# The MLP's down product: half its columns by one level of Strassen's scheme, between the blocks of the next up product

## The chip, the cores and the metric

The kernel runs on one core of one Trainium2 chip. A core has TensorE (PE) for matmuls, VectorE (DVE), ScalarE (ACT) and GpSimd (POOL) for the rest, and SyncE (SP), which issues most transfers. Each engine works through its own list of instructions in order and waits for others through semaphores. Matmul results go to PSUM, eight banks of 512 float32 columns on 128 partitions, from where DVE or ACT must copy them out; everything else lives in SBUF. The metric is the time of one execution in microseconds (us).

## The reference

Two decoder layers over 256 tokens of width 2048, each with a token mixer (mLSTM in layer 0, gated DeltaNet in layer 1), cross-attention into 256 memory tokens, and an MLP; each part stands between two RMS norms and is added to the residual. The change is in the MLP:

```python
D_MODEL = 2048; SEQ = 256; D_FF = 4 * D_MODEL        # 8192 features

def sq_relu_mlp(h, w_up, w_down):
    u = jax.nn.relu(h @ w_up)
    return (u * u) @ w_down

        h = rms_norm(x, g[4])
        x = x + rms_norm(sq_relu_mlp(h, w_up[i], w_down[i]), g[5])
```

## The kernel before

All matmuls run in fp32r, a reduced float32 format. To keep float32 accuracy every operand is split into a high part (a cast to fp32r) and a low part (the rest), and a product is three matmuls: high x high, high x low, low x high. Weights come from HBM as float32 (`raw`), in units of 128 x 2048 numbers; ACT makes `hi` by a cast (L101) and DVE makes `lo` by a subtraction (L102), each in two halves of 128 x 1024. The class `Weights` holds the list of all units in the order of their use (`plan`). When a unit is taken, those up to two further on are begun; there are three buffers each of `hi` and `lo` and four half-unit buffers of `raw`, so a unit's cast waits until the unit three before it has been used up by TensorE, and its transfer until a `raw` half is free.

A feature is a row of the hidden layer. The up product makes feature blocks of 128 features x 256 tokens (`prod_feat`, keys `up`): 16 blocks of the width are contracted, each by one matmul of 512 columns (L363: weights' high part against the high and low parts of `h` side by side) and one of 256 (L369: low part against high). Four feature blocks stand in four PSUM banks at once. Their evacuation (`relu2`, then `join`) is ACT copy `h_up` (L498), DVE addition `j_up` (L500), DVE relu and square in one (L1030), ACT cast (L264) and DVE subtraction (L265) into `u`.

The down product (`prod_tok`, key `down`) goes the other way: 128 tokens at a time are the stationary operand, 512 output columns the moving one, with three matmuls for each feature block, token half and column group (L437 to L439). There are four column groups, `y0` to `y3`. The MLP works in NQ = 4 chunks of 2048 features: up for the chunk, then down for the chunk, whose result is added to `y` (L557). A short extra matmul (`apart`, L365) stands between one chunk's down and the next one's up. The last chunk's down product runs inside `out_proj` (layer 0) or with the output's stores (layer 1), where the closing norm, the residual and, in layer 0, the first products of the next stage are woven in.

PSUM banks come in two kinds: five buffers of `acc` and three of `ps` (functions `acc` and `psum`). The order on each engine is set by the order of the code, with the splits of weights moved ahead by priority, and a scheduler that places each instruction.

Of the kernel before, what the change touches and what calls it, by code (L numbers as in the profile page):

```python
# [25 lines left out]
GDN_QKV, GDN_Z = 8192, 4096  # L26
XA_H, XA_DH = 4, 128
D_FF = 8192
NQ = 4
FQ = D_FF // NQ  # L30
COL_MEM, COL_HEAD, COL_GDN, COL_CONV = 192, 208, 224, 256
SOLVE_FROM = 6


class Weights:
# [10 lines left out]
    def add(self, key, w, k0, kn, n0, nn, tall=False):  # L46


        kk, un = (kn, P) if tall else (UK * P, UN)
        for n in range(n0, n0 + nn, un):  # L50
            w_n = min(un, n0 + nn - n)
            for k in range(k0, k0 + kn, kk):
                self.plan.append((key, w[k : min(k + kk, k0 + kn), n : n + w_n]))

    def begin(self, place=None):


        nc = self.nc
        if self.done == len(self.plan):
            return []  # L60
        key, src = self.plan[self.done]
        k, n = src.shape
        kb, i = k // P, self.done
        un = UN * UK // kb
        hi, lo, tiles, halves = [], [], [], []

        def take_tiles():
            if place:
                for j in range(kb):
                    for to, t in zip((hi, lo), place(j)):  # L70
                        to.append(t)
                return
            tiles.append(self.hi.tile([P, kb, un], F32R, tag="hi", name=f"hi{i}"))
            tiles.append(self.lo.tile([P, kb, un], F32R, tag="lo", name=f"lo{i}"))
            for to, t in zip((hi, lo), tiles):
                to += [t[:, j, :] for j in range(kb)]

        hb = kb // 2
        for k0 in range(0, kb, hb):
            raw = self.raw.tile([P, hb, un], F32, tag="raw", name=f"raw{i}_{k0}")  # L80
            nc.sync.dma_start(raw[:, :, :n], src[k0 * P : (k0 + hb) * P, :].rearrange("(kb p) n -> p kb n", p=P))

            def split(follow=None, k0=k0, raw=raw):
                if k0 == 0:
                    take_tiles()
                if not place:
                    ht, lt = tiles
                if kb == KB and n < P:
                    h_, l_ = ht[:, k0 : k0 + hb, 0:n], ht[:, k0 : k0 + hb, n : 2 * n]
                    a = nc.scalar.copy(h_, raw[:, :, :n])  # L90
                    return a, nc.vector.tensor_tensor(l_, raw[:, :, :n], h_, ALU.subtract)
                if place:
                    for j in range(hb):
                        h_ = hi[k0 + j][:, :n]
                        a = nc.scalar.copy(h_, raw[:, j, :n])
# [5 lines left out]
                a = nc.scalar.copy(h_, raw[:, :, :n])  # L101
                return a, nc.vector.tensor_tensor(l_, raw[:, :, :n], h_, ALU.subtract)  # L102

            halves.append(split)
        self.ready.append((key, hi, lo, kb, n))
        self.done += 1
        return halves

    def prefetch(self, n):
        while self.done < min(len(self.plan), self.taken + n):  # L110
            for half in self.begin():

                with self.tc.high_priority(offset=self.first):
                    ins = half()
                if self.splits is not None:
                    self.splits.append(ins[1])

    def take(self, key, ahead=None):
# [9 lines left out]
def trunk(ctx: ExitStack, tc, x, mem, norm_g, mem_norm_g, w_mem_kv, w_xq, w_xo, w_up, w_down,  # L128
# [87 lines left out]
    def acc(name):  # L216
        return ps.tile([P, 512], F32, tag="acc", bufs=5, name=name)
# [291 lines left out]
    def new_u(n=KB):  # L509
        return [acts.tile([P, 2 * T], F32R, tag=f"u{k}", name=f"u{k}") for k in range(n)]  # L510
# [23 lines left out]
    class Post:  # L534
# [105 lines left out]
        def split(self, half):  # L640
            self.order(*half(self.order))
# [382 lines left out]
        V.scalar_tensor_tensor(s2, s2, EPS, s2, ALU.mult, ALU.mult)  # L1024
        return s2

    def relu2(u):
        def ev_up(f, a):
            d = join(a, "up")
            V.scalar_tensor_tensor(d, d, 0.0, d, ALU.max, ALU.mult)  # L1030
            if f == 0:
                u.extend(new_u())
            split_into(u[f], d)

        return ev_up

    def mlp(l, lead):
        h = lead.h
        for c in range(NQ):
            u = []  # L1040
            prod_feat("up", h, KB, relu2(u), lead=None if c else lead, apart=last_of_down if c else None)
            if c == 0:
                post = Post(l, 5, (1, 0) if l == 0 else None)
            if c < NQ - 1:
                last_of_down = prod_tok("down", u, 4, lambda ch, t, a: post.add(ch, t, a, c == 0))
# [12 lines left out]
        prod_tok("down", u, 4, last, split=True)  # L1058
# [485 lines left out]
```

## Time and profile before

| what | value |
|---|---|
| median of 3 runs | 2859.65 us (2859.62 to 2866.31) |
| span of the profiled execution | 2861.4 us (the page gives no other total of it) |
| TensorE busy | 2837.7 us, 99% of the span |
| DVE busy | 1775.2 us, 62% |
| ACT busy | 1447.6 us, 51% |
| mean granted TensorE clock | 0.997 |
| MLP of layer 0, of layer 1 | 507 to about 1195 us, 2150 us to the end |
| moved by DMA | 562.31 MB, mean 197 GB/s |

A row of groups has: line, engine, operation, output <- inputs, shapes, count | busy us in all, mean ns of one | idle time of the engine just before them, and what ended it. A row of the timeline has: start, length, engine, line, operation. Lengths of matmuls overlap, so their rate is read from starts.

### The profile page before, as it was taken

What the parts mean: (1) busy time and instruction counts of PE and PEld (TensorE: products, weight loads), DVE (VectorE), ACT (ScalarE), POOL (GpSimd) and SP (SyncE); (2) the same over time, 40 slices, a digit from 0 to 9 for tenths busy, and PEclk for the clock granted to TensorE, in tenths of its full rate; (3) what the DMA queues carried; (4) which work ended last, traced back from release to release, by engine and by line L of the source; (5) the groups of instructions that cost most, each with busy time, mean ns of one, the idle gap of its engine ahead of it and who ended that gap; (6) DMA issues with size and microseconds to landing.
All of it is one profiled execution on the core that took longest, in us unless ns stands there. A gap on an engine that the chain in (4) does not pass through costs nothing.

```text
span 2861.4 us, 41169 instructions
## 1 busy us (share of the span) xinstructions
PE 2837.7 (99%) x15876; PEld 2426.8 (85%) x15876; DVE 1775.2 (62%) x2715; ACT 1447.6 (51%) x2201; POOL 170.3 (6%) x365
## 2 busy tenths in 40 slices
PE   9999999999999999999999999999999999999998
PEld 8888888888888888888888998888888888888887
DVE  6555657754645555687877895555577545555565
ACT  7354547644434444466765554544476444344443
POOL 0000000000000000002211114230000000000000
PEclk9999999999999999999999999999999999999999
DMA  8545565555555666658878778665655655656664
GB/s 281 182 148 176 188 201 172 167 191 191 191 192 191 191 191 191 218 158 233 245 217 227 209 219 262 196 202 197 208 160 177 189 193 190 193 190 192 192 191 155
DMA packets 379860, 562.31 MB, mean 197 GB/s; under 512 B 24672, under 2 KB 158640, under 8 KB 378384
## 3 DMA queue, kind: packets, MB, share of 16 engines
q1 hardware_dynamic: 362304, 505.02, 56.7%
q0 software_dynamic: 16464, 53.58, 5.8%
q8 instruction: 124, 2.03, 0.3%
q10 hardware_dynamic: 896, 1.09, 0.1%
q14 instruction: 72, 0.59, 0.1%
HBM read 534.38 MB, written 25.23 MB: 196 GB/s over the span
## 4 chain that ended last, share of the span: by engine, by line
PE 85%; DMA 5%; DVE 4%; ACT 4%; issue 2%; POOL 0%; DVEq 0%; ACTq 0%; SPq 0%; POOLq 0%
PE up L363 15%; PE down L437 8%; PE down L438 8%; PE down L439 8%; PE up L369 8%; PE gv L386 2%; PE o L363 2%; PE g_out L438 2%; PE g_out L439 2%; PE g_out L437 2%; ACT hi L101 2%; PE gz L437 1%; PE gz L439 1%; PE gz L438 1%; DVE lo L102 1%
## 5 line engine op out<-in xcount | busy, mean ns | idle before, releaser
L102 DVE TENSOR_TENSOR lo<-raw,hi 128x1024 fp32r<-128x1024 f32 (+1 forms) x924 | 1096.5, 1220 | 821.9 <-ACT hi L101 820.8
L101 ACT CAST hi<-raw 128x1024 fp32r<-128x1024 f32 (+1 forms) x924 | 932.5, 1049 | 905.3 <-PE down L439 311.1
L363 PE MATMUL up<-h,hi 128*128 128x512 f32 x1952 | 678.0, 392 | 1.5 <-DVE j_up L500 1.5
L369 PE MATMUL up<-h,lo 128*128 128x256 f32 x1952 | 544.9, 280 | 0.7 <-DVE lo L102 0.6
L363 PEld LDWEIGHTS up<-h,hi 128*128 128x128 f32 x1952 | 364.9, 187 | 81.8 <-issue 2.1
L439 PE MATMUL down<-hi,u 128*128 128x512 f32 x1024 | 398.5, 389 | 0.0
L438 PE MATMUL down<-lo,u 128*128 128x512 f32 x1024 | 398.5, 389 | 0.0
L437 PE MATMUL down<-hi,u 128*128 128x512 f32 x1024 | 398.4, 389 | 0.0
L369 PEld LDWEIGHTS up<-h,lo 128*128 128x128 f32 x1952 | 368.7, 189 | 3.0 <-DVE lo L102 2.3
L437 PEld LDWEIGHTS down<-hi,u 128*128 128x128 f32 x1024 | 192.2, 188 | 40.0
L439 PEld LDWEIGHTS down<-hi,u 128*128 128x128 f32 x1024 | 192.2, 188 | 40.0
L438 PEld LDWEIGHTS down<-lo,u 128*128 128x128 f32 x1024 | 192.2, 188 | 39.7
L437 PE MATMUL gz<-hi,h 128*128 128x512 f32 x256 | 103.0, 402 | 0.0
L439 PE MATMUL gz<-hi,h 128*128 128x512 f32 x256 | 102.4, 400 | 0.0
L438 PE MATMUL gz<-lo,h 128*128 128x512 f32 x256 | 102.4, 400 | 0.0
L1104 DVE SCALAR_TENSOR_TENSOR cv<-pad,cols,cv 128x256 f32<-128x256 f32 x192 | 92.0, 481 | 15.7 <-ACT cv L1102 12.3
L386 PE MATMUL gv<-h,hi 128*128 128x512 f32 x256 | 89.5, 394 | 0.0
L386 PE MATMUL gk<-h,hi 128*128 128x512 f32 x256 | 89.0, 392 | 0.0
L363 PE MATMUL o<-h,hi 128*128 128x512 f32 x256 | 89.0, 391 | 0.0
L264 ACT CAST u<-j_up 128x256 fp32r<-128x256 f32 x128 | 48.9, 406 | 57.9 <-DVE j_up L1030 57.9
L390 PE MATMUL gv<-h,hi 128*128 128x256 f32 x256 | 72.8, 284 | 0.0
L498 ACT COPY h_up<-up 128x256 f32<-128x256 f32 x128 | 47.1, 368 | 50.5 <-PE up L369 48.2
(473 smaller groups left out, 4582.5 us busy)
## 6 DMA issues: line engine op xcount, KB each, us to landing
raw<-in_w_up SPq DMA_DIRECT2D x256, 512.0 KB, 4.0
raw<-in_w_down SPq DMA_DIRECT2D x256, 512.0 KB, 4.5
raw<-in_gdn_w_in SPq DMA_DIRECT2D x192, 512.0 KB, 5.0
raw<-in_mlstm_w_in SPq DMA_DIRECT2D x96, 512.0 KB, 4.0
raw<-in_gdn_w_out SPq DMA_DIRECT2D x64, 512.0 KB, 4.7
raw<-in_mlstm_w_out SPq DMA_DIRECT2D x32, 512.0 KB, 4.7
at_d<-at POOLq DMA_DIRECT2D x8, 1536.0 KB, 7.6
ab<-at_d POOLq DMA_DIRECT2D x16, 768.0 KB, 5.0
```

The lines of the kernel that those rows point to most:

```text
L101: a = nc.scalar.copy(h_, raw[:, :, :n])
L102: return a, nc.vector.tensor_tensor(l_, raw[:, :, :n], h_, ALU.subtract)
L264: a = S.copy(dst[:, 0:T], src)
L363: m = PE.matmul(a[:fw], wh, srcs[kk][:, :], start=(kk == 0), stop=False, skip_group_check=True)
L369: PE.matmul(a[:fw, T:], wl, srcs[kk][:, 0:T], start=False, stop=(kk == nk - 1), skip_group_check=True)
L386: PE.matmul(a, hi[k], srcs[k][:, :], start=(k == 0), stop=False, skip_group_check=True)
L390: m = PE.matmul(a[:, 0:T], hi[k], srcs[k][:, 0:T], start=(k == 0), stop=False)
L437: PE.matmul(a, sh, hi[j], start=(kk == 0), stop=False)
L438: PE.matmul(a, sh, lo[j], start=False, stop=False)
L439: end[0] = PE.matmul(a, sl, hi[j], start=False, stop=(kk == nk - 1))
L498: S.copy(h[:n], a[:n, T:])
L1104: V.scalar_tensor_tensor(c, pad[:, j : j + T], w[j], c, ALU.mult, ALU.add)
```

## The change

The MLP works in NQ = 8 chunks of 1024 features (FK = 8 feature blocks). For chunks 0 to 6 the down product of two of the four column groups (`y0`, `y1`) is done by one level of Strassen's scheme in Winograd's form. A pair of feature blocks against two column groups, with the two token halves, is a 2 x 2 times 2 x 2 block product: seven block products into seven PSUM banks `m0` to `m6` (five of `acc`, two of `ps`) in place of eight. They need four sums of blocks of `u` (`ssum`, function `combos`, split into `sh` and `sl`) and four of the weights (`tsum`, function `begin_pair`, split into `hi` and `lo`). The four pairs of a chunk are accumulated in the banks; then the seven banks are added to (or, in the first chunk, copied into) seven float32 tiles, and after the last chunk seven additions make the four results of them.

The seven products of a pair of chunk c-1 stand between feature blocks of the up product of chunk c: up block f, then three products ("part 0", raw weights and `t3`), up block f+1, then four products ("part 1"). Each up block has a single `ps` bank, its weights come as a "tall" unit (2048 rows x 128 columns), and its evacuation is different: ACT copies all 512 columns (`both`), DVE adds the halves, ACT does relu, square and the cast, DVE the subtraction. After these four pairs the other two column groups of chunk c-1 follow as before. The down product of chunk 7, all four groups, runs as before in `out_proj` or with the stores, now over 8 feature blocks instead of 16. `apart` is no longer used.

```diff
-NQ = 4
+NQ = 8
 FQ = D_FF // NQ
+FK = FQ // P
...
+        def split():
...
+            if part:
+                t = sums[0]
+                for j in (0, 2):
+                    nc.scalar.copy(ht[:, j : j + 2, :], t[:, j : j + 2, :])
+                for j in (0, 2):
+                    sub(lt[:, j : j + 2, :], t[:, j : j + 2, :], ht[:, j : j + 2, :])
+                return
+            (b11, b12), (b21, b22) = ([r[:, j, :] for j in range(2)] for r in rows_)
+            t = self.tsum.tile([P, UK, UN], F32, tag="tsum", name=f"tsum{i}")
+            sums.append(t)
+            nc.scalar.copy(ht[:, 0, :], b11)
+            nc.scalar.copy(ht[:, 1:3, :], rows_[1])
+            sub(t[:, 0, :], b12, b11)
+            sub(lt[:, 0, :], b11, ht[:, 0, :])
+            sub(lt[:, 1:3, :], rows_[1], ht[:, 1:3, :])
+            sub(t[:, 2, :], b22, b12)
+            sub(t[:, 1, :], b22, t[:, 0, :])
+            sub(t[:, 3, :], t[:, 1, :], b21)
...
-        for c in range(NQ):
-            ws.add("up", w_up[l], 0, D, c * FQ, FQ)
-            ws.add("down", w_down[l], c * FQ, FQ, 0, D)
+        ws.add("up", w_up[l], 0, D, 0, FQ)
+        for c in range(1, NQ):
+            for f in range(0, FK, 2):
+                ws.add("up", w_up[l], 0, D, c * FQ + f * P, P, tall=True)
+                ws.add_pair("down2", w_down[l], (c - 1) * FQ + f * P, 0)
+                ws.add("up", w_up[l], 0, D, c * FQ + (f + 1) * P, P, tall=True)
+                ws.plan[-2:] = ws.plan[:-3:-1]
+            ws.add("down", w_down[l], (c - 1) * FQ, FQ, 2 * UN, D - 2 * UN)
+        ws.add("down", w_down[l], D_FF - FQ, FQ, 0, D)
...
+        def evac(self, f, b):
+            if f % 4 == 0:
+                self.full = self.mp.tile([P, 4, T], F32, tag="u32", name="u32")
+            both = self.mp.tile([P, 2, T], F32, tag="both", bufs=2, name="both")
+            S.copy(both, b.t.rearrange("p (h x) -> p h x", h=2))
+            d = t256("j_up")
+            V.tensor_tensor(d, both[:, 0, :], both[:, 1, :], ALU.add)
+            S.activation(d, d, AF.Relu)
+            full = self.full[:, f % 4, :]
+            S.activation(full, d, AF.Square)
+            split_into(self.u[f], full)
+            if self.combine and f % 4 == 3:
+                self.combos(f // 4)
+
+        def combos(self, half):
...
+            V.tensor_tensor(s_[:, 0], a21, a22, ALU.add)
+            V.tensor_tensor(s_[:, 2], a11, a21, ALU.subtract)
+            V.tensor_tensor(s_[:, 1], s_[:, 0], a11, ALU.subtract)
+            V.tensor_tensor(s_[:, 3], a12, s_[:, 1], ALU.subtract)
+            S.copy(h_, s_)
+            V.tensor_tensor(l_, s_, h_, ALU.subtract)
+            self.forms.append((h_, l_))
...
+        for c in range(1, NQ):
+            nxt = Half(mp, c % 2, c < NQ - 1)
+            banks = [acc(f"m{i}") for i in range(5)] + [psum(f"m{i}") for i in range(5, 7)]
+            for f in range(FK):
+                hi, lo, nk, _ = ws.take("up")
+                a = psum("up")
+                for k in range(nk):
+                    PE.matmul(a, hi[k], h[k][:, :], start=(k == 0), stop=False, skip_group_check=True)
+                    PE.matmul(a[:, T:], lo[k], h[k][:, 0:T], start=False, stop=(k == nk - 1), skip_group_check=True)
+                nxt.evac(f, Bank(a, True))
+                j, part = f // 2, f % 2
+                hi, lo, nf, _ = ws.take("down2")
...
+                for i in range(nf):
+                    (sh, sl), a = lhs[i], banks[to[i]]
+                    PE.matmul(a, sh, hi[i], start=(j == 0), stop=False)
+                    PE.matmul(a, sh, lo[i], start=False, stop=False)
+                    PE.matmul(a, sl, hi[i], start=False, stop=(j == FK // 2 - 1))
+                if j == FK // 2 - 1:
+                    for i in to:
+                        if c == 1:
+                            S.copy(kept[i], banks[i])
+                        else:
+                            V.tensor_tensor(kept[i], banks[i], kept[i], ALU.add)
+            if c == NQ - 1:
...
+            prod_tok("down", cur.u, 2, lambda ch, t, a: post.add(ch + 2, t, a, c == 1))
+            cur = nxt
```

How this stands on the engines, at three places of layer 0. Numbers after names are buffers; that of a weight tile is its unit. First TensorE, before: two up blocks follow each other with nothing between (end of block 7, start of block 8, in different banks).

```order
L363 MATMUL up7_6383<-h14_4825,hi121_6420 128x512
L369 MATMUL up7_6383<-h14_4825,lo121_6421 128x256
L363 MATMUL up7_6383<-h15_4826,hi121_6420 128x512
L369 MATMUL up7_6383<-h15_4826,lo121_6421 128x256
L363 MATMUL up8_6580<-h0_4602,hi122_6462 128x512
L369 MATMUL up8_6580<-h0_4602,lo122_6463 128x256
```

TensorE now, in chunk 3: the end of up block 4 (unit 158), part 0 of the third pair (unit 159, banks `m0` to `m2`), and the start of up block 5 (unit 160).

```order
L1151 MATMUL up_7832<-h15_4837,hi158_7739 128x512
L1152 MATMUL up_7832<-h15_4837,lo158_7740 128x256
L1164 MATMUL m0_7517<-hi159_7799,u12_6751 128x512
L1165 MATMUL m0_7517<-lo159_7800,u12_6751 128x512
L1166 MATMUL m0_7517<-hi159_7799,u12_6751 128x512
L1164 MATMUL m1_7518<-hi159_7799,u13_6752 128x512
L1165 MATMUL m1_7518<-lo159_7800,u13_6752 128x512
L1166 MATMUL m1_7518<-hi159_7799,u13_6752 128x512
L1164 MATMUL m2_7519<-hi159_7799,sh1_7326 128x512
L1165 MATMUL m2_7519<-lo159_7800,sh1_7326 128x512
L1166 MATMUL m2_7519<-hi159_7799,sl1_7327 128x512
L1151 MATMUL up_7899<-h0_4602,hi160_7826 128x512
```

What moved: nine matmuls of the previous chunk's down product now stand between two up blocks, which share a bank. Second, ACT before, while an up stage runs: evacuations of a group of four blocks, then only casts of weights.

```order
L264 CAST u6_6337<-j_up_6558 128x256
L498 COPY h_up_6563<-up7_6383 128x256
L101 CAST hi124_6574<-raw124_2_6572 128x1024
L264 CAST u7_6338<-j_up_6565 128x256
L101 CAST hi125_6620<-raw125_0_6616 128x1024
L101 CAST hi125_6620<-raw125_2_6618 128x1024
```

ACT now, at the same place as above (`up_7832` is block 4, `up_7899` block 5): the combinations' cast `sh0`, one cast of unit 161, the copy of block 4, and so on.

```order
L1118 CAST sh0_7787<-ssum_7786 128x1024
L86 CAST hi161_7874<-tsum159_7801 128x1024
L1098 COPY both_7866<-up_7832 128x512
L86 CAST hi161_7874<-tsum159_7801 128x1024
L154 CAST hi162_7893<-raw162_0_7889 128x1024
L1101 ACTIVATE j_up_7868<-j_up_7868 128x256
L154 CAST hi162_7893<-raw162_8_7891 128x1024
L1103 ACTIVATE u32_7865<-j_up_7868 128x256
L323 CAST u4_7513<-u32_7865 128x256
L93 CAST hi163_7944<-raw163_0_7940 128x512
L1098 COPY both_7932<-up_7899 128x512
```

What moved: the copy that frees the up bank now stands behind two casts of other data, and relu and square are ACT's. Third, DVE before, in an up stage:

```order
L102 TENSOR_TENSOR lo124_6575<-raw124_2_6572,hi124_6574 128x1024
L1030 SCALAR_TENSOR_TENSOR j_up_6565<-j_up_6565 128x256
L265 TENSOR_TENSOR u7_6338<-j_up_6565,u7_6338 128x256
L102 TENSOR_TENSOR lo125_6621<-raw125_0_6616,hi125_6620 128x1024
L102 TENSOR_TENSOR lo125_6621<-raw125_2_6618,hi125_6620 128x1024
```

DVE now, from the last work for block 3 to the next evacuation; the last of the four `ssum` rows (L1117; the first, L1115, stands earlier) is the one that `sh0` on ACT reads.

```order
L324 TENSOR_TENSOR u3_7512<-u32_7567,u3_7512 128x256
L1114 TENSOR_TENSOR ssum_7786<-u32_7567 128x256
L155 TENSOR_TENSOR lo160_7827<-raw160_0_7822,hi160_7826 128x1024
L1116 TENSOR_TENSOR ssum_7786<-ssum_7786,u32_7567 128x256
L155 TENSOR_TENSOR lo160_7827<-raw160_8_7824,hi160_7826 128x1024
L1117 TENSOR_TENSOR ssum_7786<-u32_7567,ssum_7786 128x256
L1119 TENSOR_TENSOR sl0_7788<-ssum_7786,sh0_7787 128x1024
L82 TENSOR_TENSOR lo161_7875<-tsum159_7801,hi161_7874 128x1024
L1100 TENSOR_TENSOR j_up_7868<-both_7866 128x256
L82 TENSOR_TENSOR lo161_7875<-tsum159_7801,hi161_7874 128x1024
```

What moved: sums and splits for the scheme stand among the weight splits, in front of the addition that the next evacuation needs.

More of the change, by code (lines that the diff above doesn't have):

```diff
@@ L52, in add, with add_pair, begin_pair @@
             for k in range(k0, k0 + kn, kk):
-                self.plan.append((key, w[k : min(k + kk, k0 + kn), n : n + w_n]))
+                self.plan.append((key, w[k : min(k + kk, k0 + kn), n : n + w_n], None))
+    def add_pair(self, key, w, k0, n0):
+        src = w[k0 : k0 + 2 * P, n0 : n0 + 2 * UN]
+        self.plan += [(key, src, 0), (key, src, 1)]
+    def begin_pair(self, key, src, part):
+        nc, i = self.nc, self.done
+        nf = 4 if part else 3
+        if part == 0:
+            rows_ = []
+            for r in range(2):
+                rows_.append(self.raw.tile([P, 2, UN], F32, tag="raw", name=f"raw{i}_{r}"))
+                nc.sync.dma_start(rows_[r], src[r * P : (r + 1) * P, :].rearrange("p (b n) -> p b n", b=2))
+            self.rows = rows_
+            self.sums = []
+        rows_, sums = self.rows, self.sums
+        hi, lo = [], []
+        def split():
+            ht = self.hi.tile([P, UK, UN], F32R, tag="hi", name=f"hi{i}")
+            lt = self.lo.tile([P, UK, UN], F32R, tag="lo", name=f"lo{i}")
+            hi.extend(ht[:, j, :] for j in range(nf))
+            lo.extend(lt[:, j, :] for j in range(nf))
+            sub = lambda d, a, b: nc.vector.tensor_tensor(d, a, b, ALU.subtract)
+            if part:
[16 more added lines that the diff above has]
+            sub(t[:, 3, :], t[:, 1, :], b21)
+        self.ready.append((key, hi, lo, nf, UN))
+        self.done += 1
+        return [split]
     def begin(self, place=None):
@@ L60, in begin @@
             return []
-        key, src = self.plan[self.done]
+        key, src, part = self.plan[self.done]
+        if part is not None:
+            return self.begin_pair(key, src, part)
         k, n = src.shape
@@ L114, in prefetch @@
                     ins = half()
-                if self.splits is not None:
+                if self.splits is not None and ins:
                     self.splits.append(ins[1])
@@ L1025, in mlp_bias, with __init__, form, block @@
         return s2
[L1027 to L1035, printed above, removed]
+    class Half:
+        def __init__(self, mp, par, combine):
+            self.mp, self.combine, self.forms = mp, combine, []
+            self.u = [acts.tile([P, 2 * T], F32R, tag=f"u{par * FK + k}", name=f"u{par * FK + k}") for k in range(FK)]
+        def evac(self, f, b):
[12 more added lines that the diff above has]
+        def combos(self, half):
+            a = self.full.rearrange("p (j i) (t x) -> p j i t x", j=2, t=2)
+            (a11, a21), (a12, a22) = ([a[:, :, i, t, :] for t in range(2)] for i in range(2))
+            s_ = self.mp.tile([P, 4, 2, P], F32, tag="ssum", name="ssum")
+            h_, l_ = (self.mp.tile([P, 4, 2, P], F32R, tag=f"s{n}{half}", name=f"s{n}{half}") for n in "hl")
+            V.tensor_tensor(s_[:, 0], a21, a22, ALU.add)
[5 more added lines that the diff above has]
+            self.forms.append((h_, l_))
+        def form(self, i, j):
+            h_, l_ = self.forms[j // 2]
+            return h_[:, i, j % 2, :], l_[:, i, j % 2, :]
+        def block(self, k, t):
+            u = self.u[k]
+            return u[:, t * P : (t + 1) * P], u[:, T + t * P : T + (t + 1) * P]
@@ L1037, in mlp @@
     def mlp(l, lead):
+        mp_stack = ExitStack()
+        mp = ws.tsum = mp_stack.enter_context(tc.tile_pool(name="mp", bufs=1))
         h = lead.h
[L1039 to L1045, printed above, removed]
+        cur = Half(mp, 0, True)
@@ new lines, in mlp @@
+        prod_feat("up", h, FK, cur.evac, lead=lead)
+        post = Post(l, 5, (1, 0) if l == 0 else None)
+        y = post.y
+        m = [tmp.tile([P, 512], F32, tag="pair", bufs=3, name=f"m{i}") for i in range(3)]
+        m1, m6, m7 = m
+        c11, c21, c12, m5 = (y[ch][:, t, :] for ch in range(2) for t in range(2))
+        kept = [m1, c11, c12, m5, m6, m7, c21]
+        for c in range(1, NQ):
[10 more added lines that the diff above has]
+                hi, lo, nf, _ = ws.take("down2")
+                if part == 0:
+                    lhs = [cur.block(2 * j, 0), cur.block(2 * j + 1, 0), cur.form(3, j)]
+                    to = (0, 1, 2)
+                else:
+                    lhs = [cur.form(0, j), cur.form(1, j), cur.form(2, j), cur.block(2 * j + 1, 1)]
+                    to = (3, 4, 5, 6)
+                for i in range(nf):
[7 more added lines that the diff above has]
+                            S.copy(kept[i], banks[i])
+                        else:
+                            V.tensor_tensor(kept[i], banks[i], kept[i], ALU.add)
+            if c == NQ - 1:
+                for d, a, b, op in ((c11, c11, m1, ALU.add), (m6, m6, m1, ALU.add), (m7, m7, m6, ALU.add),
+                                    (c21, m7, c21, ALU.subtract), (c12, c12, m6, ALU.add), (c12, c12, m5, ALU.add),
+                                    (m5, m5, m7, ALU.add)):
+                    V.tensor_tensor(d, a, b, op)
+            prod_tok("down", cur.u, 2, lambda ch, t, a: post.add(ch + 2, t, a, c == 1))
+            cur = nxt
@@ L1046, in mlp @@
+        mp_stack.close()
+        u = cur.u
         post.bias = mlp_bias(lead.x_rms)
```

## The prediction

> **What bounds the kernel now.** I read the page first, then the stretches of the two MLP stages, then TensorE's waits, then single instructions.
>
> ```profile
> span 2861.4 us, 41169 instructions
> PE 2837.7 (99%) x15876; PEld 2426.8 (85%) x15876; DVE 1775.2 (62%) x2715; ACT 1447.6 (51%) x2201; POOL 170.3 (6%) x365
> ...
> 600.00:1190.00 590.00, 590.00 (x2973) 502.95 (x2972) 322.05 (x395) 255.28 (x334) 0.00 (x0) 1.00 0.61 192
> 2300.00:2840.00 540.00, 540.00 (x2748) 461.42 (x2747) 299.49 (x374) 234.09 (x309) 0.00 (x0) 1.00 0.60 190
> ...
> PE up L363 <- DVE j_up L500: 1.5, 1, 1.5
> ```
>
> The page's engine line, two stretches inside the MLP stages of both layers (busy us of PE, weight loads, DVE, ACT, POOL, then granted clock, DMA share and GB/s), and TensorE's only long wait around an up or down product (it is in the lead-in of layer 0). In the MLP stages TensorE has work in every microsecond at full clock, while DVE is busy for 55% and ACT for 43%. So a matmul that goes saves its full slot, for as long as nobody else comes late.
>
> A busy share says nothing of the slot, since matmuls overlap. That comes from start times:
>
> ```profile
> 599.95 0.27 PE L369 MATMUL up<-h,lo 128*128 128x256 f32 x1
> 600.06 0.40 PE L363 MATMUL up<-h,hi 128*128 128x512 f32 x1
> 600.26 0.37 ACT L498 COPY h_up<-up 128x256 f32<-128x256 f32 x1 [0.58 <-PE up L369]
> 602.49 0.39 PE L363 MATMUL up<-h,hi 128*128 128x512 f32 x1
> ...
> 689.89 0.38 PE L365 MATMUL apart<-ones,ident 128*128 128x128 f32 x2
> 690.03 0.48 PE L363 MATMUL up<-h,hi 128*128 128x512 f32 x1
> 690.35 0.28 PE L369 MATMUL up<-h,lo 128*128 128x256 f32 x1
> ...
> 780.95 0.39 PE L437 MATMUL down<-hi,u 128*128 128x512 f32 x1
> 784.35 0.39 PE L437 MATMUL down<-hi,u 128*128 128x512 f32 x1
> ```
>
> Between the last two rows lie 15 matmuls of 512 columns (five triples of L437 to L439): 3.40/15 = 0.2267 us each. Between 600.06 and 602.49 lie seven pairs of an up product (512 and 256 columns): 0.347 us a pair, so 16 pairs, one feature block, take 5.55 us. The ACT row starts 0.20 us after TensorE has gone on to the next block: that is how late an evacuation can begin.
>
> **The change, part by part.**
>
> *Removed.* For each pair of feature blocks the first two down columns took 2 blocks x 2 columns x 2 token halves x 3 = 24 matmuls; now 7 products x 3 = 21. There are 4 pairs in each of 7 chunks and 2 layers: 168 matmuls x 0.2267 = 38.1 us, all on TensorE's full path. The six `apart` matmuls (two records each) go too: 690.35 - 689.89 is 0.46 us where 0.227 would stand without, so 6 x 0.23 = 1.4 us. Up products keep their matmuls.
>
> *Added work.* The nearest rows by shape:
>
> ```profile
> L102 DVE TENSOR_TENSOR lo<-raw,hi 128x1024 fp32r<-128x1024 f32 x920 | 1092.6, 1221 | 820.7 <-ACT hi L101 819.5
> L500 DVE TENSOR_TENSOR j_up<-up,h_up 128x256 f32<-128x256 f32 x128 | 50.8, 416 | 0.0
> L557 DVE TENSOR_TENSOR y<-down,y 128x512 f32<-128x512 f32 x48 | 33.0, 687 | 30.3 <-PE down L439 30.3
> L101 ACT CAST hi<-raw 128x1024 fp32r<-128x1024 f32 x920 | 929.1, 1050 | 904.2 <-PE down L439 311.1 <-PE up L363 181.3 <-issue 146.7
> L264 ACT CAST u<-j_up 128x256 fp32r<-128x256 f32 x128 | 48.9, 406 | 57.9 <-DVE j_up L1030 57.9
> L557 ACT COPY y<-down 128x512 f32<-128x512 f32 x16 | 9.4, 588 | 22.7 <-PE down L439 22.7
> L95 ACT CAST xwh<-raw 128x512 fp32r<-128x512 f32 x12 | 6.8, 617 | 2.8 <-DMA raw<-in_w_up 2.5 <-DMA raw<-in_gdn_w_in 0.3
> ```
>
> One chunk (8 up blocks, 4 pairs, two down columns) on TensorE: 8 x 5.55 + 84 x 0.2267 + 96 x 0.2267 = 44.4 + 19.0 + 21.8 = 85.2 us. On DVE: up splits 16 x 1.221; per pair five ops of 512 and three of 1024, 4 x 7.10; evacuations 16 x 0.416; two sets of combinations 2 x (4 x 0.416 + 1.221); seven bank additions 7 x 0.687; down splits 8 x 1.221 and four additions of 0.687: 19.5 + 28.4 + 6.7 + 5.8 + 4.8 + 9.8 + 2.7 = 77.7 us, 91%. On ACT: 16 x 1.05 + 4 x (0.617 + 3 x 1.05) + 8 x 1.05 + evacuations 8 x (0.588 + 3 x 0.406) + 2 x 1.05 = 56.8 us, 67%. Neither is the bound by its sum; what counts is the order in which they stand.
>
> *The new wait.* `m5` and `m6` hold two of the three `ps` banks through a whole chunk, so every up block has one and the same bank. Up block f+1 cannot start until ACT has copied block f out (`both`); the cover is the products between them: 9 x 0.2267 = 2.04 us after an even block, 12 x 0.2267 = 2.72 us after an odd one. After an odd block the copy stands behind one cast of 512: 0.20 + 0.62 + 0.59 = 1.41 us, covered. After an even one it stands behind one cast of 1024 (`hi161` in the order shown): 0.20 + 1.05 + 0.59 = 1.84 us, covered with 0.2 us to spare, if ACT is idle by then. It isn't after block 4, where the cast `sh0` of the combinations is in front, which waits for the last of four sums on DVE.
>
> So I follow DVE's queue to there. Time 0 is the end of up block 1; by TensorE's slots block 2 ends at 8.27, block 3 at 15.86, block 4 at 24.13, and block 5 is due at 26.17. The first split of unit 157 needs the slots that block 2 frees: cast 8.47 to 9.52, and from there DVE always has something ready: seven ops of 1024, eight of 256, five of 512, up to the sum that `sh0` needs. With full durations these are 7 x 1.221 + 8 x 0.416 + 5 x 0.687 = 15.3 us, `sh0` starts at 24.9, and `both` ends at 24.9 + 1.05 + 1.05 + 0.59 = 27.6: block 5 starts 1.45 us late. But a full DVE queue runs tighter:
>
> ```profile
> 1620.00:1660.00 40.00, 40.00 (x337) 40.00 (x337) 39.83 (x72) 21.08 (x32) 1.77 (x9) 1.00 0.73 198
> ...
> 1640.95 0.42 DVE L1099 TENSOR_TENSOR pad<-gv,rb 128x256 f32<-128x256 f32 x1
> 1641.29 0.61 DVE L1305 TENSOR_TENSOR solve_w<-tm,solve_w 128x440 f32<-128x440 f32 x1
> 1641.81 2.35 DVE L102 TENSOR_TENSOR lo<-raw,hi 128x1024 fp32r<-128x1024 f32 x2
> 1644.08 0.61 DVE L1308 TENSOR_TENSOR tm<-tm,solve_w 128x440 f32<-128x440 f32 x1
> ...
> 1664.28 0.69 DVE L1305 TENSOR_TENSOR solve_w<-tm,solve_w 128x510 f32<-128x510 f32 x1
> 1664.89 0.42 DVE L1099 TENSOR_TENSOR pad<-gv,rb 128x256 f32<-128x256 f32 x1
> ...
> 608.48 2.01 ACT L101 CAST hi<-raw 128x1024 fp32r<-128x1024 f32 x2 [0.68 <-PE down L439]
> ```
>
> Starts follow each other after 1.135 us (two of 1024 in 2.27), 0.34 (256) and 0.61 (512), and two ACT casts end 2.01 us after the first began, 0.96 apart. That gives 7.95 + 2.72 + 3.05 + 0.2 for operations that read what was just written = 13.9 us, `sh0` at 23.5, `both` done at 26.0: 0.15 us early. The ends are 0 and 1.45 us, at 12 places (chunks 1 to 6 of both layers; chunk 7 makes no combinations). The nearest row is the saturated stretch, where TensorE loses nothing beside a DVE at 39.83 of 40 us; I take 0.35 us for hand-overs not counted: 12 x 0.35 = 4.2 us.
>
> The Trainium skill says in "VectorE: DVE Perf Modes", section "The DRAIN you can't avoid", that after each operation the next doesn't start until the pipeline is empty, though it adds that one that isn't held starts earlier. Read strictly, that is the 1.45 us end. The rows above start earlier than that by 0.07 to 0.09 us an operation, so the trace sides with the exception.
>
> *The seven bank additions* stand on DVE's queue ahead of a split and of the next evacuation, and wait for the last pair's products. The first is ready 0.9 us after block 6; replaying the queue on from there, the split behind it (`lo165`) is done at 45.2, needed at 48.4. Cover: 3 us. In chunk 1 they are ACT copies, in like places. The down columns behind take 21.8 us with 12.5 us of DVE work, in which it catches up.
>
> *Transfers.* Up weights now come in rows of 512 B, not 2 KB.
>
> ```profile
> raw<-in_w_up SPq DMA_DIRECT2D x256, 512.0 KB, 4.0
> raw<-in_gdn_w_in SPq DMA_DIRECT2D x192, 512.0 KB, 5.0
> ...
> q1 hardware_dynamic: 26668, 13.45, 72.8%
> ...
> q1 hardware_dynamic: 7356, 14.18, 59.6%
> ```
>
> The DeltaNet's up-like weights are loaded in that shape: 5.0 us to landing. The last two rows are the queue in 1570 to 1640 (512 B rows) and 700 to 774 us (2 KB rows): 264 and 322 GB/s at full share. Half of 16.8 MB a chunk each way is 57 us of 85.2. The tightest landing is the second half of unit 160: its slot comes free at 14.5, its cast must end by 21.8, so 6.3 us may pass. Covered by 1.3 us.
>
> *The rest.* The lead-in of each layer has the same up matmuls and four evacuations in one burst as before; the last down product is 8 steps instead of 16 with the same splits at its end, so the ACT and DVE work of the closing norm is twice as dense. I take 1.5 us a layer, 3 in all (ends -1.5, the wait above gone, and +8).
>
> *Sum*, for the profiled execution: 2861.4 - 38.1 - 1.4 + 4.2 + 3.0 = 2829.1 us. The page has no other total than its span, which is 1.75 us above the median of 2859.65; taking that off, 2827 us.
>
> **The rivals.**
>
> *DVE's operations don't overlap* where each waits for ACT: 12 x 1.45 = 17.4 us instead of 4.2, 2841 us. For it: most of the splits do wait for a cast. Against: the saturated stretch. This is also what the strict reading of that section of the Trainium skill would give.
>
> *512 B rows land late.* At 8 us instead of 5 the second half of unit 160 is 1.7 us behind, and `both` 1.5: 12 x 1.5 = 18 us, 2845 us with the rest. Against: 5.0 us in the same shape.
>
> *DVE becomes the bound (slower).* The place is the pair stretch, where each split waits for a cast that waits for TensorE to free a slot:
>
> ```profile
> DVE lo L102 <- ACT hi L101: 248.3, 107, 3.6
> DVE y L557 <- PE down L439: 11.1, 8, 1.4
> ```
>
> (waits of DVE in 600 to 1190 us: total, times, longest.) One such wait is 2.3 us, one for a finished bank 1.4. If four of the first and five of the second stay in each chunk although the queue is full, DVE needs 77.7 + 9.3 + 6.9 = 93.9 us, 8.7 over TensorE's 85.2; times 14 chunks 122 us, 2861.4 - 39.5 + 122 + 3 - 1.75 = 2945 us. It decides from 11 of these 16 us on: then 14 x 3.4 = 48 us eat the gain and 0.3% more. Against: these waits are for something TensorE does at a fixed time, and shrink when DVE comes later.
>
> That matmuls don't go away is no rival: the program has 174 fewer, 168 and 6.
>
> **How the numbers follow.** My forecast, stalls of at most 14 us in all (up to 2834), 0.50; no overlap 0.27; late rows 0.05; DVE the bound in part, within 0.3% of before, 0.08; and in full, slower, 0.10. About 0.3% (8.6 us) is what a measurement of this kernel can tell from no change. The first three are all faster by more: 0.82. Without any stall and with the lead-in's wait gone it is 2861.4 - 39.5 - 1.5 - 1.75 = 2819, the low end less 1; the high end takes in both middle cases with 5 us for the layers' ends: 2850.
>
> **What would show it.** Right: TensorE's span in a chunk near 85 us; the only repeated wait is of the up product's first matmul for ACT `both`, under 0.5 us, once a chunk; DVE near 90%, ACT near 67% there; rows of `in_w_up` landing in about 5 us. Wrong: that wait over 1 us or after every even block; TensorE waiting for `lo` of DVE; casts waiting for DMA; or gaps at the lead-in and the closing norm above 3 us.

## The result, and the profile after

The changed kernel takes 2837.24 us (median of 4 runs, 2836.02 to 2838.13), the kernel before beside it 2859.64 us: a ratio of 0.9918, 95% interval 0.9904 to 0.9932. The forecast was 2827 us. The sign and the cause were right; 10 of the 32.6 us that were forecast did not come. The head of the page, and two of its rows on DMA issues:

```profile
span 2835.9 us, 41595 instructions
PE 2815.1 (99%) x15696; PEld 2396.1 (84%) x15696; DVE 2101.0 (74%) x3177; ACT 1672.4 (59%) x2603; POOL 170.4 (6%) x365
...
raw<-in_w_up SPq DMA_DIRECT2D x256, 512.0 KB, 4.7
raw<-in_w_down SPq DMA_DIRECT2D x256, 512.0 KB, 5.1
```

There are 180 matmuls fewer (168, and six times two records of `apart`), and DVE and ACT are busier. TensorE is still busy all the time, so either the matmuls got longer or they wait. All waits of TensorE within up blocks, products and down columns of the whole run:

```profile
PE up L422 <- ACT both L1098: 0.4, 1, 0.4
PE up L1152 <- DVE lo L155: 0.4, 1, 0.4
```

One is in the lead-in, one in the first interleaved chunk. The wait that the prediction looked for, of an up block for `both` once a chunk, isn't there. The stretch of one chunk, from the start of up block 0 to that of the next chunk (columns as in the prediction):

```profile
642.72:729.06 86.34, 86.34 (x437) 73.02 (x436) 69.96 (x91) 52.85 (x75) 0.00 (x0) 1.00 0.65 193
```

A chunk takes 86.35 us (starts 642.73 and 729.07 give 86.34), not 85.2, at full clock and without a gap. So the matmuls themselves stand further apart. TensorE's starts at two places show by how much: one up block and one part each, late and early.

```profile
563.57 0.39 PE L1151 MATMUL up<-h,hi 128*128 128x512 f32 x1
...
572.54 0.40 PE L1151 MATMUL up<-h,hi 128*128 128x512 f32 x1
...
578.18 0.40 PE L1164 MATMUL m<-hi,u 128*128 128x512 f32 x1
...
642.73 0.39 PE L1151 MATMUL up<-h,hi 128*128 128x512 f32 x1
...
648.37 0.40 PE L1164 MATMUL m<-hi,u 128*128 128x512 f32 x1
...
650.46 0.39 PE L1151 MATMUL up<-h,hi 128*128 128x512 f32 x1
...
656.11 0.39 PE L1164 MATMUL m<-hi,sh 128*128 128x512 f32 x1
...
658.87 0.39 PE L1151 MATMUL up<-h,hi 128*128 128x512 f32 x1
```

An up block takes 5.64 us (648.37 - 642.73) where the kernel before took 5.55; a part of 9 products 2.09 instead of 2.04 and one of 12 products 2.76 to 2.77 instead of 2.72. The down columns behind are unchanged: 96 matmuls in 21.76 us, 0.2267 each. Eight blocks and eight parts make 1.15 us a chunk, 16.1 us in 14 chunks. The starts in the trace, from one 512-column matmul of an up block to the next (a pair), show a pattern:

```
ns from pair to pair, first ten of a block
before, block at 695.67               347 346 347 347 346 347 347 346 347 347
after, 563.57 (behind a wait)         976 351 351 347 347 346 347 347 346 347
after, 572.54 (straight on)           352 342 351 360 350 350 360 350 350 360
after, 666.61 (straight on)           340 350 361 349 350 361 349 350 361 349
```

All later blocks that follow products repeat the last row to within 1 ns, whatever DVE, ACT and the transfers do meanwhile; the block that began behind a wait does not show it. That gave the first theory: TensorE has more than one steady rhythm in a stream that alternates 512 and 256 columns, and which one it falls into is set by how it enters.

### The profile page after: what moved, and what is told of

It reads as the page before. It is cut to its first block, busy times and chain, and to the rows that moved or that the text cites. A ratio compares the mean times of both kernels' runs of the same rounds, so it can differ in the third digit from the quotient of the medians.

```text
span 2835.9 us, 41595 instructions
## 1 busy us (share of the span) xinstructions
PE 2815.1 (99%) x15696; PEld 2396.1 (84%) x15696; DVE 2101.0 (74%) x3177; ACT 1672.4 (59%) x2603; POOL 170.4 (6%) x365
## 4 chain that ended last, share of the span: by engine, by line
PE 40%; DVE 6%; ACT 3%; DMA 2%; issue 2%; POOL 0%; DVEq 0%; ACTq 0%; POOLq 0%
PE up L1151 7%; PE up L1152 4%; DVE lo L155 2%; PE down L496 2%; PE down L497 2%; PE down L498 2%; PE g_out L497 2%; PE g_out L496 2%; PE g_out L498 2%; PE m L1165 2%; PE m L1164 2%; PE m L1166 2%; PE gz L496 1%; PE gz L498 1%; PE gz L497 1%
## 5 line engine op out<-in xcount | busy, mean ns | idle before, releaser
L155 DVE TENSOR_TENSOR lo<-raw,hi 128x1024 fp32r<-128x1024 f32 x812 | 966.3, 1220 | 327.7 <-ACT hi L154 324.9
L154 ACT CAST hi<-raw 128x1024 fp32r<-128x1024 f32 x812 | 827.1, 1047 | 479.6 <-PE down L498 96.7
L1152 PE MATMUL up<-h,lo 128*128 128x256 f32 x1792 | 503.4, 281 | 0.4 <-DVE lo L155 0.4
L496 PE MATMUL down<-hi,u 128*128 128x512 f32 x576 | 224.2, 389 | 0.0
L497 PE MATMUL down<-lo,u 128*128 128x512 f32 x576 | 224.1, 389 | 0.0
L498 PE MATMUL down<-hi,u 128*128 128x512 f32 x576 | 224.1, 389 | 0.0
L82 DVE TENSOR_TENSOR lo<-tsum,hi 128x1024 fp32r<-128x1024 f32 x112 | 136.8, 1221 | 82.6 <-ACT hi L86 82.5
L86 ACT CAST hi<-tsum 128x1024 fp32r<-128x1024 f32 x112 | 117.6, 1050 | 131.9 <-PE up L1151 96.6
L496 PEld LDWEIGHTS down<-hi,u 128*128 128x128 f32 x576 | 108.1, 188 | 22.5
L498 PEld LDWEIGHTS down<-hi,u 128*128 128x128 f32 x576 | 108.1, 188 | 22.5
L497 PEld LDWEIGHTS down<-lo,u 128*128 128x128 f32 x576 | 108.1, 188 | 22.3
L82 DVE TENSOR_TENSOR lo<-raw,hi 128x512 fp32r<-128x512 f32 x112 | 103.6, 955 | 0.0
```

The lines of the kernel that those rows point to most:

```text
L82: sub = lambda d, a, b: nc.vector.tensor_tensor(d, a, b, ALU.subtract)
L86: nc.scalar.copy(ht[:, j : j + 2, :], t[:, j : j + 2, :])
L496: PE.matmul(a, sh, hi[j], start=(kk == 0), stop=False)
L497: PE.matmul(a, sh, lo[j], start=False, stop=False)
L498: end[0] = PE.matmul(a, sl, hi[j], start=False, stop=(kk == nk - 1))
L1152: PE.matmul(a[:, T:], lo[k], h[k][:, 0:T], start=False, stop=(k == nk - 1), skip_group_check=True)
```

## The experiments

Runs differ by several us in code that no experiment edits: from the last down matmul of layer 0 to the first up matmul of layer 1 it took 918.5 to 929.2 us. Without waits, however, nearly all successive chunks of a run take the same time to 0.01 us. So each experiment is read by one chunk; 14 times the difference is its effect.

**The order within an up block.**

```diff
 for k in range(nk):
     PE.matmul(a, hi[k], h[k][:, :], ...)
+for k in range(nk):
     PE.matmul(a[:, T:], lo[k], h[k][:, 0:T], ...)
```

> The order of an up block in chunks 1 to 7: first its 16 matmuls of 512 columns (hi), then its 16 of 256 (lo), no longer by turns. Nothing else changes. Theory (entry): the long slots of the changed kernel come from how TensorE enters a stream that alternates 512 and 256 columns straight out of a stream of 512: once in it goes on at 349, 350, 361 ns a pair, after a gap at 346 and 347. Without alternation a block takes 16 x 226.7 + 16 x 120 = 5.55 us instead of 5.64, so 112 blocks give back 11 us: 2826 us; with the products behind them at 226.7 ns too, 15.6 us: 2822 us. Rival (load): DVE, ACT or the transfers slow TensorE's reads in these stretches; then the order is worth nothing, 2837 us. Rival (banks): seven open accumulators slow it; 2837 us too.

Measured: 2832.11 us, the kernel before beside it 2864.56; ratio 0.989 (0.9872 to 0.9909). One chunk, and the starts of one block and the part behind it:

```profile
642.70:728.25 85.55, 85.55 (x438) 73.11 (x436) 71.08 (x92) 54.43 (x75) 0.00 (x0) 1.00 0.66 196
```

```profile
666.28 0.39 PE L1151 MATMUL up<-h,hi 128*128 128x512 f32 x1
...
671.82 0.39 PE L1165 MATMUL m<-hi,sh 128*128 128x512 f32 x1
...
674.60 0.39 PE L1151 MATMUL up<-h,hi 128*128 128x512 f32 x1
```

The block takes 5.54 us (16 at 226.7 and 16 at 119.5 ns), the products behind it 2.78, no less than before. 0.80 us a chunk is 11.2 us: the theory's first number, and not its second. DVE and ACT do as much as in the changed kernel, so load isn't the cause. The order on ACT and DVE also came out a little differently (`both` mostly starts 0.2 us behind its block, not 1.04), but TensorE waits for neither in both kernels.

**A gap ahead of each block.**

```diff
 a = psum("up")
+PE.matmul(a[:, 0:P], ident, ones, start=True, stop=True)
 for k in range(nk):
```

> One small matmul (ident by ones, 128 columns, two records) is set ahead of each of the 112 interleaved up blocks, as the kernel before had one ahead of each of its later up products. Theory (entry): it costs 0.23 us as there, and the block behind it then goes at 346 to 347 ns a pair from its second pair on, 0.09 us less: 112 x 0.14 = 15 us slower than the changed kernel, 2852 us, with the pairs in the trace as the proof. Rivals (load, banks): the pairs stay at 349, 350, 361 ns, and the time is 2837 + 112 x 0.23 = 2863 us.

Measured: 2848.82 us.

```profile
643.61:731.13 87.52, 87.52 (x454) 74.59 (x453) 70.38 (x92) 53.17 (x75) 0.00 (x0) 1.00 0.63 188
```

1.17 us a chunk more, 16.4 us, close to the theory's 15. The pairs are the proof: 438 346 347 347 346 347 347 in one block, 439 350 343 350 344 350 343 in another, 346.7 on average in both. So it is in all 108 blocks with the small matmul right ahead. The scheduler set those of the first two blocks of each layer into the lead-in; the second of these follows products straight on, and its pairs are 340 350 361 again. Nothing but the entry is different. Whether it is the gap that counts or the small matmul itself, this run doesn't separate.

**The scheme's sums left out.**

```diff
-t = sums[0]                       # part 1: splits of the four sums
-...
+ht, lt = sums                     # part 1: the slices of part 0 again
...
-sub(t[:, 0, :], b12, b11)         # and the three other sums
-if self.combine and f % 4 == 3: self.combos(f // 4)
```

> Same matmuls in the same order, into the same seven banks, but the work of the scheme on DVE and ACT is left out: neither the sums of weight blocks nor those of feature blocks are formed, and the products take plain splits of the blocks in their place. DVE falls by about 30 us a chunk, ACT by 10. Theory (entry): pairs at 349, 350, 361 ns as before, 2836 us. Rival (load): the slots go back to 346.7 and 226.7 ns, 2837 - 15.6 = 2822 us. Rival (banks): unchanged, 2837 us.

Measured: 2831.32 us.

```profile
642.70:728.83 86.13, 86.13 (x437) 72.98 (x436) 47.92 (x58) 43.87 (x65) 0.00 (x0) 1.00 0.65 196
```

DVE falls from 70 to 48 us a chunk, ACT from 53 to 44, and the up blocks stay at 5.64 us with 340 350 361 349 350 361. Load on DVE and ACT is out. But 0.21 us a chunk did go, and the starts say where: in the products.

```
ns from start to start, a part of 9 and one of 12 products
changed, 664.51   233 236 228 233 230 235 234 234 231
changed, 672.25   228 236 234 231 235 233 235 230 227 227 226 227
sums left out     232 236 229 232 231 227 226 227 227
sums left out     232 236 228 233 231 226 227 227 226 227 227 226
```

After an up block the first five matmuls are long in any case (26 ns together). In the changed kernel the others are long too; in the part of 12 up to the last one whose next weights are a form (`sh` or `sl`).

**Ordinary products between the blocks.** Eight block products of a pair instead of seven, into four banks, with plain splits:

```diff
-lhs = [cur.form(0, j), cur.form(1, j), cur.form(2, j), cur.block(2 * j + 1, 1)]
+for ch in range(2):
+    for t in range(2):
+        (sh, sl), a = cur.block(f, t), banks[2 * ch + t]
```

> The interleaving alone: between the up blocks stand the eight ordinary block products of a pair (12 matmuls behind each up block, into four banks, the up blocks by turns in three others) instead of the seven. TensorE has 168 matmuls more than the changed kernel, 38.1 us. Theory (entry): interleaving alone makes the slots long, 2837 + 38 = 2875 us, that is 15 us slower than the kernel before, with pairs at 349, 350, 361 ns. Rivals (load of the scheme's sums, seven open banks): the slots are 346.7 and 226.7 ns as in the kernel before, 2837 + 38 - 15.6 = 2860 us.

Measured: 2871.39 us.

```profile
647.77:736.62 88.85, 88.85 (x449) 75.24 (x448) 48.50 (x55) 44.31 (x65) 0.00 (x0) 1.00 0.62 189
```

The same matmuls in unbroken stages would be 8 x 5.547 + 192 x 0.2267 = 87.9 us. Interleaving alone costs 0.95 us a chunk, 13.3 us in all, with 5.64 us a block; neither seven open banks nor Strassen's sums are needed for it. In total it is 6.8 us behind the kernel before rather than the expected 15: it has no `apart` (1.4 us), and the edges of the stages gain (below).

**Two and two.** `hi`, `hi`, `lo`, `lo`:

> Up blocks by turns of two: hi, hi, lo, lo. Theory (entry into alternation): the loss hangs on the change from 256 to 512 columns, after which some matmuls are 6 to 9 ns long; with half as many changes the block lies between 5.54 (one change) and 5.64 us (sixteen), near 5.59, 2837 - 5 = 2832 us. Rival (any run of two of the same length breaks the cycle): 5.54 us, 2826 us. Rival (it is as long as by ones): 5.64 us, 2837 us.

Measured: 2832.08 us.

```profile
644.62:730.28 85.66, 85.66 (x438) 72.69 (x436) 70.75 (x92) 52.87 (x75) 0.00 (x0) 1.00 0.65 195
```

A block takes 5.564 us: between the two, but nearer to 5.54 than expected. Turns of two lose a quarter of what turns of one lose ((5.564 - 5.538) of (5.64 - 5.538)), and behind them a part of 9 takes 2.077 us instead of 2.093: its first two matmuls are long, by 10 ns together, and not five.

**The place of the forms.** The products' excess needed another theory. Of the tiles in `mp`, TensorE reads `sh` and `sl` alone. In the compiled program they start at a multiple of 64 B, while weights, `h` and `u` start 32 B past one. A tile of 32 B at the head of `mp` moves the forms into the phase of the rest; the order of TensorE and ACT stays the same, instruction by instruction.

```diff
 mp = ws.tsum = mp_stack.enter_context(tc.tile_pool(name="mp", bufs=1))
+V.memset(mp.tile([P, 8], F32, name="pad_mp"), 0.0)
```

> The changed kernel with a tile of 32 B a partition at the start of the pool mp, so that sums and forms (ssum, sh, sl, tsum, both) start at byte 32 of a 64-byte line, as weights, features and u do already, and no longer at byte 0. Theory (address): the matmuls ahead of and with a formed operand, which take 231 to 235 ns where the same places take 227 without the forms, go back to 227: products of a pair 4.81 us instead of 4.86, 2.7 us in all, 2833 us; up pairs stay at 349, 350, 361 ns. Rival (the forms are slow for another reason, as that ACT and DVE work beside them): unchanged, 4.86 us and 2836 us.

Measured: 2837.1 us, a chunk of 86.13, and a part of 12 from 674.80 to 677.54:

```profile
645.36:731.49 86.13, 86.13 (x437) 72.97 (x436) 68.87 (x91) 52.95 (x75) 0.00 (x0) 1.00 0.64 191
```

```profile
674.80 0.40 PE L1165 MATMUL m<-hi,sh 128*128 128x512 f32 x1
...
677.54 0.39 PE L1152 MATMUL up<-h,hi 128*128 128x512 f32 x1
```

Per chunk 0.21 us less, 3 us in all: parts of 2.07 and 2.75 us, the same slots as with the sums left out. (The single total doesn't show 3 us.) The two runs with all tiles at multiples of 64 B tell whether it is the line or the difference that counts:

> The changed kernel's order (hi and lo by turns) with all big tiles at multiples of 64 B. Theory (entry): the byte at which tiles start has no part in the long pairs; 349, 350, 361 ns stay, products at 4.81 us, as with the shift of mp alone, 2835 us. Rival (address): the pairs come from moving data and weights that lie across 64-byte lines, and go to 346.7 ns, 10 us less, 2825 us.

> Up blocks first hi, then lo, and all big tiles start at a multiple of 64 B (a tile of 32 B a partition at the head of the constants and one at the head of mp); before, all but mp's stood at byte 32 of a 64-byte line. Theory (address): with weights, moving data and forms in the same phase the slots of the products fall to 227 ns and those of 256 columns from 120 towards 113: 2.7 to 15 us below the same order unaligned (2832 us), 2817 to 2829 us. Rival: the start of a tile within 64 B is nothing to TensorE, 2832 us with the same slots.

```profile
644.26:730.40 86.14, 86.14 (x438) 72.98 (x436) 70.20 (x93) 52.84 (x75) 0.00 (x0) 1.00 0.64 196
```

(the first of the two.) By turns: 2828.71 us, 86.13 a chunk, pairs still 350 361, parts of 2.07 and 2.75 us. First `hi`, then `lo`: 2825.41 us, 85.33 a chunk, 120 ns for 256 columns and not 113. (Outside the chunks read here, this order waits for `both` twice, 2.0 us together.) So all at byte 0 or all at byte 32 is the same; a mixture costs. Whether the load of a form is slowed by the weights before it or by the moving data beside it was not tried.

**Both edits together, beside the changed kernel.**

> Both edits that shortened slots, together: up blocks first hi then lo, and the tile of 32 B at the head of mp; the order of TensorE and ACT is that of the kernel with the first edit alone. Theory: up blocks 5.54 us, products of a pair 4.81 us, a chunk of 44.3 + 19.3 + 21.8 = 85.4 us, 14 x 0.95 = 13.3 us below the changed kernel run beside it, ratio to the kernel before 0.987. Rival (the two gains aren't additive, or what comes earlier meets a new wait, as 2.0 us did in the aligned one): 10 us below.

> The changed kernel itself, on the same chip and beside the same runs of the kernel before as the best version, so that the two can be compared: 0.992 of the kernel before, as in the first comparison (0.9904 to 0.9932).

Measured: 2827.04 us, ratio 0.9882 (0.9867 to 0.9897); the changed kernel 2838.79 us, 0.9916 (0.9902 to 0.9929). The intervals don't meet: this version is faster than both kernels.

```profile
642.68:728.02 85.34, 85.34 (x438) 73.15 (x436) 70.14 (x91) 54.34 (x75) 0.00 (x0) 1.00 0.65 196
```

1.01 us a chunk, 14.2 us; 11.75 us between the medians. What is left over the prediction's 85.2 us is 0.13 us.

The second trace of the changed kernel shows one thing more. In layer 1's first up stage, which no products interrupt, TensorE stops for a moment near 2160 us in both executions (0.71 us from one start to the next in the first trace, 0.41 in this one), and then goes on like this, first trace first:

```profile
2169.72 0.40 PE L422 MATMUL up<-h,hi 128*128 128x512 f32 x1
...
2171.80 0.40 PE L422 MATMUL up<-h,hi 128*128 128x512 f32 x1
```

```profile
2169.81 0.40 PE L422 MATMUL up<-h,hi 128*128 128x512 f32 x1
...
2171.93 0.40 PE L422 MATMUL up<-h,hi 128*128 128x512 f32 x1
```

Six pairs take 2.08 us in the first trace (346.7 ns a pair) and 2.12 in this one (353.3), to the end of the stage, with the same instructions in the same order. So TensorE does have two rhythms in one and the same stream and keeps the one it is in; but a stop ahead doesn't make the short one sure, and the long one doesn't need products before it. What in the entry decides is open.

**The cover of the evacuation.**

```diff
-S.copy(both, b.t.rearrange("p (h x) -> p h x", h=2))
+for _ in range(2 if f % 2 == 0 else 1):
+    S.copy(both, b.t.rearrange("p (h x) -> p h x", h=2))
```

> The copy of an up block out of its bank (both) is done twice after every even block, so the next block may start 0.58 us later. In the changed kernel the copy was done 0.43 to 0.47 us ahead of it. Theory (the cover ends there): 56 places with a wait of ACT both of 0.12 to 0.15 us, 7 to 8 us; since a gap ahead of a block puts its pairs back to 346 or 347 ns (0.09 us less), only 2 to 3 us of it is left, 2839 us. Rival (the cover is wider, the copy's end isn't what frees the bank): no wait, 2836 us. Rival (a wait costs its full length or more, since what is queued behind it on ACT comes later too): 2844 us and above.

Measured: 2856.97 us, in the open end of the last rival. The test isn't clean: with the longer copy the order of the program itself came out differently, with five matmuls of the next part ahead of the up block. From 640 us to the end of layer 0's chunks no up block waits for `both` (before that one does, for 0.6 us). TensorE's only wait there, and one chunk:

```profile
PE m L1165 <- ACT hi L86: 3.5, 5, 1.1
```

```profile
648.92:736.73 87.81, 86.80 (x437) 72.69 (x436) 71.08 (x92) 54.74 (x79) 0.00 (x0) 1.00 0.64 192
```

Where the cover ends stays open. What it shows, longer copy and changed order together, is that ACT, 61% busy in the changed kernel, has little room at this place: the casts `hi` of the sums come late, and a chunk takes up to 1.5 us longer for 0.58 us of ACT work four times.

**More work for DVE.**

```diff
-sub(t[:, 2, :], b22, b12)
-...
+for _ in range(2):
+    sub(t[:, 0, :], b12, b11)
+    ...                           # all four sums, twice
```

> DVE forms the four weight sums of each pair twice: 16 more operations of 128x512 a chunk at 0.61 us, 9.8 us, so DVE goes from 70.4 to about 80 us of the 86.35 us of a chunk, 93%. Theory (DVE's waits shrink when it comes later): no wait of TensorE for lo, 2836 to 2838 us. Rival (DVE becomes the bound, as in the prediction: its waits for casts stay): each chunk over 86.35 us, TensorE waits for lo L82 or L155, and from 5 us a chunk on 2907 us.

Measured: 2875.3 us. One chunk, and TensorE's waits in layer 0's chunks:

```profile
648.44:738.54 90.10, 86.95 (x437) 72.81 (x436) 82.05 (x112) 54.20 (x75) 0.00 (x0) 1.00 0.63 190
```

```profile
PE down L499 <- DVE lo L157: 12.9, 9, 1.8
```

My theory fell. With DVE busy for 82 us the chunk takes 90.1 us, and TensorE waits for `lo`. A chunk takes 3.3 us more on average (88.7 to 90.6 us in all), less than the rival's 5, but of its kind; the waits that the profile names make up about 2 us of it (in the whole run 24.8 us for `lo`, 4.7 for casts `hi` of the sums). The edge lies between 71 us busy a chunk, where no such wait appears, and 82: below a full DVE.

## Why the prediction was right in sign and short in size

*Removed matmuls*: right. 180 records fewer, 39.5 us by the prediction's prices.

*Durations of what stays*: this step failed, and it was not named as a risk. 5.55 us for an up block and 0.2267 us for a product were read from stretches where each followed its own kind. In the new order nearly every block follows a stream of 512 columns without a gap, and every part a stream with 256. That costs 1.15 us a chunk, 16.1 us. The runs split it: about 0.8 us from the alternation in the up blocks (gone with `hi` first), 0.21 from forms that start in another phase (gone with the shift), and 0.13 that is left: the five long matmuls after each block make 0.21, and blocks of 5.54 instead of 5.55 us give some of it back. In the kernel before, `apart` stood at the entry into all up products but the two of the lead-ins, and behind it the short rhythm held through all six stages; the change took it away.

Both costs stood in the trace of the kernel before, at places that the prediction didn't read:

```profile
524.06 0.40 PE L363 MATMUL up<-h,xwu 128*128 128x512 f32 x1
...
526.18 0.40 PE L363 MATMUL up<-h,xwu 128*128 128x512 f32 x1
...
778.87 0.39 PE L437 MATMUL down<-hi,u 128*128 128x512 f32 x1
...
780.95 0.39 PE L437 MATMUL down<-hi,u 128*128 128x512 f32 x1
```

Between the first two rows, in layer 0's lead-in, lie six pairs of an up product: 2.12 us, the long rhythm. The third row is the first matmul of a down product right behind an up product: nine products take 2.08 us, not 2.04. Seven of the eight down products begin so. The prediction read its 15 products from 780.95 on, where the long ones end.

The Trainium skill gives in "TensorE: Matmul & The Clock Gate", section "Back-to-back issue gap", one distance for a length: 131 ns sustained for 512 columns, and for a matmul alone at full clock N / 2.4 + 2.5 ns, which is 216 for 512 and, as an estimate by that formula, 109 for 256. Here long runs of one length go at 226.7 and 119.5, and 241 and 120 stand in a long pair; the measurement decides, and the sequence matters. The Trainium skill's "SBUF — State Buffer", section "Operand start alignment", lets an fp32 operand start at any multiple of 4 B. It says nothing of time; in time, mixed starts cost 0.21 us a chunk here.

*The wait for `both`*: forecast 4.2 us, measured 0, the low end. ACT's queue around up block 5 of that chunk, due at 682.75:

```profile
679.67 1.05 ACT L1118 CAST sh<-ssum 128x1024 fp32r<-128x1024 f32 x1 [2.14 <-DVE ssum L1117]
680.75 1.05 ACT L86 CAST hi<-tsum 128x1024 fp32r<-128x1024 f32 x1
681.70 0.58 ACT L1098 COPY both<-up 128x512 f32<-128x512 f32 x1
```

The order is the forecast one: the cast `sh` behind the last sum, another cast, then the copy. `both` is done at 682.28, 0.47 us early, where the queue worked out in the prediction left 0.15. At the other even blocks 0.43 to 0.47 us is left, not 0.2. The 0.35 us set aside for hand-overs had no row behind it and was not needed. The first rival, that DVE's operations don't overlap, falls: a chunk's work, 77.7 us by the prediction's rows, occupies DVE for 69.96, and ACT for 52.85 instead of 56.8 (81% and 61% of the chunk, where near 90% and 67% were named).

*Late rows*: they land in 4.7 us, within the 6.3 allowed, and TensorE never waits for them. *DVE as the bound*: it didn't happen at 70 us, but the doubled sums show that it was near. The prediction let the gain go from 11 us of waits on top of 77.7 on, that is 3.5 us over TensorE's 85.2. The doubled sums bring as much by its prices (16 x 0.687 us), and a chunk grew by 3.3 us. That fits, but DVE was busy for only 82 of 90.1 us, so its mechanism, a DVE that is full, isn't shown.

*Lead-in and closing*: forecast +3, measured -3.0. From the first up to the last down matmul both layers took 711.0 + 708.8 = 1419.8 us before and 696.6 + 696.8 = 1393.4 after, 26.4 less, where the terms above give 39.5 - 16.1 = 23.4. Before, two up blocks of layer 0's first chunk took 6.2 and 7.2 us instead of 5.55; after, one block behind a wait takes 6.2. That is 1.7 us of it; the rest is left open.

*From span to time*: 1.75 us were taken off. But the profiled run of the changed kernel took 2837.68 us at a span of 2835.9, 1.8 above it, and in the other runs on record too the time is 1.7 to 2.0 us above the execution's own span. By that, the profiled execution of the kernel before took about 2863 us, 3.5 above the median: the term was scatter between executions, not a step from span to time. The difference of 10.2 us adds up to 0.1: slots +16.1, wait -4.2, edges -6.0, the stage between the layers +1.1 (925.3 and 926.5 us), span to median +3.1. That the time came out as near as this is partly luck: the wait and the edges, forecast too high, hid 10.2 us of what the slots cost.

## What to carry to other kernels

In these runs a matmul's slot depended on the sequence, not only on its shape: before work is moved between unlike streams, look for a place in the trace where the same two kinds already meet, and price the stretch from start times there. Try matmuls of one length in groups rather than by turns, and operands that TensorE reads in one stream at the same byte of 64 (here 0 and 32 were tried). When a busy engine has no waits and the time is still missing, compare its distances from start to start; a busy share can't show it.

## What the runs showed of the hardware

- TensorE kept a rhythm through streams that alternate 512 and 256 columns: 346.7 ns a pair or 353.3 (350, 350, 361). In blocks entered straight from products it was 353.3, behind a small matmul 346.7, and behind waits in the lead-ins either. The short one lasted through stages of 16 blocks.
- The first matmuls of 512 columns behind an up block were long, by 26 ns over five in the changed order with plain operands, by 42 over nine in seven places of the kernel before, and by 10 over two behind turns of two.
- Weights from tiles 32 B out of phase with the others made matmuls of 227 ns 230 to 235 ns long. Why, these runs don't show.
- TensorE waited for `lo` where DVE was busy for 82 of 90.1 us a chunk, and did not at 71 of 85.6.
